# One list for all engines: the instructions of a decoder layer noted first, then put out in a searched sequence

## The chip, the cores and the metric

The kernel runs on one core of a Trainium2 chip. A core has five engines with an instruction stream each: TensorE (PE, matrix products, with its weight loads shown as PEld), VectorE (DVE), ScalarE (ACT), GpSimd (POOL) and SyncE (SP, which only issues transfers here). They meet through semaphores alone. The metric is the device time of one execution in microseconds (us); the profile shows one execution, instruction by instruction.

## The reference

One layer of a hybrid decoder: 512 tokens, width 1024, everything in float32. Three mixers run side by side (sliding-window attention, stick-breaking attention, attention to a memory of 256 rows), each through its own gate; then an output projection, a residual, and a gated feed-forward block of width 2816.

```
u = rms_norm(h, ln_mix_pre)
qa, ka, va, qb, kb, vb, qm, gl = split(u @ w_in)          # 1024 x 5888
y_swa = swa_sink_attention(qa, ka, va, sinks, rel_bias)   # 8 heads, window 128
y_sb  = stick_breaking_attention(qb, kb, vb)              # 8 heads
mk, mv = split(rms_norm(mem, ln_mem) @ w_mem_kv)
y_mem = memory_cross_attention(qm, mk, mv)                # 4 heads
g = sigmoid(gl)
merged = g0 * (y_swa @ w_branch_swa) + g1 * (y_sb @ w_branch_sb) + g2 * (y_mem @ w_branch_mem)
h = h + rms_norm(merged @ w_out, ln_mix_post)
u = rms_norm(h, ln_ffn_pre)
h = h + rms_norm((silu(u @ w_gate) * (u @ w_up)) @ w_down, ln_ffn_post)
```

## The kernel before

Every float32 factor is split into a high half (a cast, `hi`, on ACT) and the rest (a subtraction, `lo`, on DVE), and a product is three products of halves: hi by hi, hi by lo, lo by hi (`mm3`). The large products are done in seven partial products of 2 by 2 blocks; weight sums for these are made by accumulating transfers.

A `Stream` object carries a sequence of weight units. Each unit is loaded (512 KB to a `raw` tile, issued by SP or by POOL), split into `hi` and `lo`, and used by TensorE. Attention and the softmaxes are woven in between.

The function `tile_kernel` is run once to issue all instructions. The order in which it issues them is not the order in which the engines run them: the wrapper class `Noted` (through whose line 232 every instruction is issued, so that the profile gives one line for all of them) keeps each engine's instructions in a list `seen`, and at the end of `tile_kernel` a loop ties each engine's instructions into the sequence given by `ORDER`, a dictionary with one list for each engine, by dependencies that need no semaphore (`follow`). Numbers in `ORDER` count the instructions of that engine. `PLAN` says which buffer each tile takes: `raw`, `hi`, `lo`, `fraw`, `fhi`, `flo` for weights, `ck` and `ck2` for 512 and 1024 wide tiles, `p` and `p2` for the eight PSUM banks, `s` for small ones. Which instruction must wait for which is found in the order of issue, so a buffer's users follow one another in that order, whatever `ORDER` says.

The names that matter below, all at the start of the kernel unless said otherwise:

- `WARM` = 9 matrix products on constants open TensorE's stream.
- `first_load` and `first_split` load and split the first three weight units in four pieces (`PIECE`: 1, 2, 2 and 3 of the 8 columns of 128). ACT itself issues the first piece of units 0 and 2, then loads its function table (`preload_act_table_set`).
- `gain_split` makes the halves of one of the eight slices of the input, `u[k]`: times the gain, high half by ACT, low half by DVE. They are the tiles named pair; slice 0 comes with the gains in `xg` (the tile wide), the others in tiles named xT.
- `xacc` is the sum of squares; `rstd_of` splits it (`sh_x`, `sl_x`) and adds it up over partitions by two products with ones (`on_x`).
- Much later, in the memory branch, `mem_vals` multiplies halves of the memory (`mh`, `ml`) by weights `hi`, `lo`. `seven_raw` copies a head's output (`yq`), `parts` splits it (`y11h`, `y11l`).

Of the kernel before, what the change touches and what calls it, by code (L numbers as in the profile page):

```python
# [17 lines left out]
P = 128  # L18
# [19 lines left out]
ORDER = {  # L38
    "tensor": (
# [23 lines left out]
    ),  # L63
    "vector": (
# [81 lines left out]
    ),  # L146
}
PLAN = {
    "raw": (
# [2042 lines left out]
```

## Time and profile before

| | |
|---|---|
| median of 3 timed runs | 768.8 us (768.69 to 768.93) |
| profiled execution, first to last instruction (span) | 766.9 us |
| around the span: median less span | 1.9 us |
| mean granted TensorE clock | 0.997 |
| TensorE, weight loads | 99%, 84% of the span |
| DVE, ACT, POOL | 88%, 68%, 14% of the span |
| HBM read, written | 140.38 MB, 19.40 MB |

The page gives no time of its own for the profiled execution beside the span, so the timed runs stand for it. Of the 40 slices of the span only the last has TensorE below nine tenths. A TensorE instruction is listed from its start to the modelled end of its pipeline, so neighbours overlap; the distance of two starts is what one costs in the stream. "x8" in a row of the timeline means eight like instructions in a row.

### The profile page before, as it was taken

What the parts mean: (1) busy time and instruction counts of PE and PEld (TensorE: products, weight loads), DVE (VectorE), ACT (ScalarE), POOL (GpSimd) and SP (SyncE); (2) the same over time, 40 slices, a digit from 0 to 9 for tenths busy, and PEclk for the clock granted to TensorE, in tenths of its full rate; (3) what the DMA queues carried; (4) which work ended last, traced back from release to release, by engine and by line L of the source; (5) the groups of instructions that cost most, each with busy time, mean ns of one, the idle gap of its engine ahead of it and who ended that gap; (6) DMA issues with size and microseconds to landing.
All of it is one profiled execution on the core that took longest, in us unless ns stands there. A gap on an engine that the chain in (4) does not pass through costs nothing.

```text
span 766.9 us, 11497 instructions
## 1 busy us (share of the span) xinstructions
PE 759.1 (99%) x4073; PEld 647.3 (84%) x4073; DVE 675.2 (88%) x1100; ACT 520.3 (68%) x946; POOL 104.1 (14%) x140
## 2 busy tenths in 40 slices
PE   9999999999999999999999999999999999999996
PEld 6789888778888888888888899988888888888885
DVE  7994897799989756999897799899999999999966
ACT  7662677777997758677944596566666668957552
POOL 0303242000222110010001201100000000214000
PEclk9999999999999999999999999999999999999998
DMA  8548999734799895469949958876777746859922
GB/s 277 166 142 233 332 328 254 211 111 149 185 188 192 184 203 163 112 134 210 340 128 329 209 130 240 203 191 180 204 192 203 220 142 187 171 120 216 261 75 111
DMA packets 50170, 150.06 MB, mean 196 GB/s; under 512 B 5984, under 2 KB 7952, under 8 KB 50016
## 3 DMA queue, kind: packets, MB, share of 16 engines
q1 hardware_dynamic: 34224, 94.38, 36.8%
q0 software_dynamic: 15600, 54.80, 36.1%
q8 instruction: 32, 0.52, 0.3%
q14 instruction: 26, 0.21, 0.1%
q10 hardware_dynamic: 288, 0.13, 0.1%
HBM read 140.38 MB, written 19.40 MB: 208 GB/s over the span
## 4 chain that ended last, share of the span: by engine, by line
PE 96%; DMA 1%; DVE 1%; ACT 1%; issue 0%; SPq 0%; DVEq 0%
PE bank L232 96%; DMA xT<-in_xT 1%; DMA raw<-in_w_p 0%; DVE xacc L232 0%; SPq L232 0%; ACT pair L232 0%; DVE pair L232 0%; ACT hi L232 0%; ACT xT L232 0%; DVE lo L232 0%; DVE fg L232 0%; DVE sl_x L232 0%; DVEq L2180 0%; DVE s L232 0%; ACT sqr L232 0%
## 5 line engine op out<-in xcount | busy, mean ns | idle before, releaser
L232 PE MATMUL bank<-pair,hi 128*128 128x512 f32 (+1 forms) x1008 | 254.4, 368 | 0.0
L232 DVE TENSOR_TENSOR lo<-raw,hi 128x1024 fp32r<-128x1024 f32 (+4 forms) x149 | 170.7, 1149 | 36.8 <-ACT hi L232 36.2
L232 PEld LDWEIGHTS bank<-pair,hi 128*128 128x128 f32 x1008 | 177.5, 189 | 27.0 <-ACT hi L232 0.9
L232 ACT CAST hi<-raw 128x1024 fp32r<-128x1024 f32 (+4 forms) x149 | 147.7, 998 | 73.7 <-PE bank L232 54.5
L232 PE MATMUL bank<-hi,pair 128*128 128x512 f32 (+1 forms) x628 | 196.3, 374 | 0.0
L232 PE MATMUL bank<-pair,lo 128*128 128x256 f32 (+1 forms) x752 | 154.7, 302 | 0.0
L232 PEld LDWEIGHTS bank<-hi,pair 128*128 128x128 f32 x628 | 115.3, 188 | 19.5 <-issue 0.2
L232 PEld LDWEIGHTS bank<-pair,lo 128*128 128x128 f32 x752 | 115.6, 190 | 10.9 <-DVE lo L232 0.7
L232 PE MATMUL bank<-lo,pair 128*128 128x512 f32 (+1 forms) x330 | 123.6, 375 | 0.0
L232 ACT CAST hi<-wide 128x1024 fp32r<-128x1024 f32 (+1 forms) x61 | 62.2, 1024 | 27.0 <-PE bank L232 11.3
L232 DVE TENSOR_TENSOR lo<-wide,hi 128x1024 fp32r<-128x1024 f32 (+1 forms) x61 | 71.9, 1185 | 4.6 <-ACT hi L232 4.3
L232 PEld LDWEIGHTS bank<-lo,pair 128*128 128x128 f32 x330 | 62.0, 188 | 10.1
L232 POOL DMA_DIRECT2D raw<-in_w_g x24 | 21.1, 878 | 124.4 <-DVE lo L232 106.2
L232 DVE TENSOR_TENSOR gp<-gp,bank 128x512 f32<-128x512 f32 x49 | 33.6, 687 | 4.6 <-PE bank L232 3.7
L232 ACT ACTIVATE sg<-gp 128x256 f32<-128x256 f32 x42 | 17.7, 421 | 23.0 <-DVE gp L232 22.9
L232 POOL DMA_DIRECT2D raw<-in_w_gu x15 | 13.2, 924 | 147.6 <-DMA raw<-in_w_gu 138.5
L232 ACT COPY gp<-bank 128x512 f32<-128x512 f32 x42 | 24.7, 588 | 2.1 <-DVE aq L232 1.4
L232 DVE TENSOR_TENSOR_SCAN bw<-br,bw 128x512 f32<-128x512 f32 (+3 forms) x32 | 24.6, 809 | 0.2
L232 DVE TENSOR_TENSOR gp<-gp,hp 128x512 f32<-128x512 f32 x36 | 24.7, 685 | 0.0
L232 POOL DMA_DIRECT2D wide<-in_w_gu x12 | 11.2, 934 | 84.6 <-DMA wide<-in_w_gu 76.3
L232 ACT COPY hp<-bank 128x512 f32<-128x512 f32 x36 | 21.5, 598 | 0.0
L232 PE MATMUL bank<-hi,ll 128*128 128x512 f32 x50 | 19.4, 389 | 0.0
(624 smaller groups left out, 1371.8 us busy)
## 6 DMA issues: line engine op xcount, KB each, us to landing
wide<-in_w_gu SPq DMA_DIRECT2D x31, 512.0 KB, 5.1
raw<-in_w_gu SPq DMA_DIRECT2D x26, 512.0 KB, 5.4
raw<-in_w_g POOLq DMA_DIRECT2D x24, 512.0 KB, 6.0
raw<-in_w_g SPq DMA_DIRECT2D x18, 512.0 KB, 4.2
raw<-in_w_gu POOLq DMA_DIRECT2D x15, 512.0 KB, 7.2
raw<-in_w_p SPq DMA_DIRECT2D x14, 512.0 KB, 6.3
wide<-in_w_gu POOLq DMA_DIRECT2D x12, 512.0 KB, 5.8
raw<-in_w_brt SPq DMA_DIRECT2D x9, 512.0 KB, 4.8
```

The costliest lines, as they stand in the source:

```text
L232: ins = f(*args, **kw)
```

## The change

The operations, 6328 of them (4009 on TensorE, 1068 on DVE, 876 on ACT, 136 on POOL, 239 on SP), are the same. `Noted` goes. `Notes` only notes each call (`Op`) in one `Program`, tiles that don't exist yet are noted as `View`s, and at the end `put_out` issues all of them along one list, `ORDER`, whose numbers count the operations of all engines in the order of noting. Each engine is tied to that sequence as before, and waits are now found in the order of that list. A `ck` tile is made when its first user is put out. `ORDER` and all of `PLAN` are new; the `after`, `behind` and `high_priority` hints are taken out.

```
-ORDER = {
-    "tensor": (
-        "0-18 21 19-20 22-24 27 25-26 28-529 538-561 572-575 580-588 642 562-564 566-567 576-579 530-537 613-620 569 "
...
+ORDER = (
+    "15-16 12 18 17 19 13 1 3 33 35 37 40 263 2 4 20 639 36 39 24 0 21 5 34 339 303 335 25 196 371 267 22 631 299 "
+    "41 38 6-10 640 716 11 720 375 94 97 100 95 98 101 42-43 93 96 14 48-49 44-45 99 23 26 29 102 28 27 30 103 "
+    "192 105-107 104 31-32 90 193-194 74 46-47 108-110 50-51 111 114 117 112 115 118 113 116 119 75-76 56-59 "
...
+class Program:
+    def put_out(self, nc, order, follow):
+        real = lambda x: x.real() if isinstance(x, View) else x
+        last, out = {}, set()
+        for n in order or range(len(self.ops)):
+            op = self.ops[n]
+            assert all(b.at in out for b in op.behind)
+            out.add(n)
+            args = [real(x) for x in op.args]
+            ins = getattr(getattr(nc, op.engine), op.name)(*args, **{k: real(x) for k, x in op.kw.items()})
+            if op.engine in last:
+                follow(ins, last[op.engine])
+            last[op.engine] = ins
...
+class Notes:
...
         def call(*args, **kw):
-            ins = f(*args, **kw)
-            self.seen.append(ins)
-            return ins
+            op = Op(len(self.program.ops), self.engine, name, args, kw)
+            self.program.ops.append(op)
+            return op
...
         if kind == "ck" and n < SINGLES:
-            return pool.tile(shape, dt, tag=f"ck{n}", name=name, bufs=1)
+            return View(once(lambda: pool.tile(shape, dt, tag=f"ck{n}", name=name, bufs=1)))
...
-    for e, text in ORDER.items():
-        seen, last = getattr(nc, e).seen, None
-        for part in text.split():
-            a, _, b = part.partition("-")
-            for k in range(int(a), int(b or a) + 1):
-                if last is not None:
-                    follow(seen[k], seen[last])
-                last = k
+    order = []
+    for part in ORDER.split():
+        a, _, b = part.partition("-")
+        order += range(int(a), int(b or a) + 1)
+    program.put_out(tc.nc, order, follow)
```

The numbers of the list that are spoken of below, counted in the order of noting:

| numbers | operations |
|---|---|
| 3 to 11 | the nine warming products |
| 12, 13; 15, 16 | ACT's loads of piece 1 of units 0 and 2; SP's of `xg` and of piece 1 of unit 1 |
| 14 | ACT's function table |
| 33, 35, 37; 34, 36, 38 | casts of piece 1 of units 0, 1, 2; their low halves (128 wide) |
| 39 and 40; 41 | high half of `u[0]`, by DVE and by ACT; low half |
| 42, 44, 46; 43, 45, 47 | casts of piece 2 of units 0, 1, 2; their low halves (256 wide) |
| 48, 49; 50, 51 | `u[1]`, high and low; `u[2]`, high and low |
| 74 | the first square, to `xacc` |
| 93 to 101; 102 to 110 | products with `u[0]`; with `u[1]`, nine each |
| 165, 166; 167, 168 | `sh_x`, `sl_x`; the two products with ones |
| 1003, 1004; 1069, 1070 | cast and low half of one weight unit of `mem_vals`, and of the next |
| 1090, 1091; 1092, 1093 | `y11h`, `y11l`; the two copies `yq` of the same bank |
| 1154 | the first product that reads what 1004 wrote |

Set side by side, engine by engine, the two sequences differ little. Of TensorE's operations 1253 of 4009 keep their place and the mean distance is 3.8 places; on DVE 286 of 1068 and 1.9 places; on ACT 274 of 876 and 1.7. The products with ones go from places 81 and 82 of TensorE's stream to 95 and 96 (from 0). Runs of transposes among TensorE's products go from 42 to 83, for the same number of transposes; the places where a 256-wide product follows a 512-wide one go from 81 to 127. TensorE's last 25 products keep their sequence.

More of the change, by code (lines that the diff above doesn't have):

```diff
@@ L1 @@
 import math
-from contextlib import ExitStack, nullcontext
+from contextlib import ExitStack
 import numpy as np
@@ L220 @@
-class Noted:
-    def __init__(self, engine):
-        self.engine, self.seen = engine, []
+ORDER = (
[207 rows of a table added]
+)
+PLAN = {
+    "raw": (
+        "1 0 2 0 3 2 1 3 3 0 2 3 1 1 0 2 3 1 3 2 0 3 1 3 1 0 2 1 3 0 2 1 0 3 2 1 0 3 2 0 1 3 1 3 1 3 2 0 2 0 2 0 1 3 "
+        "2 0 1 3 2 0 1 0 1 0 1 3 2 0 1 3"
+    ),
+    "hi": (
+        "0 1 2 0 3 2 1 2 0 1 2 0 3 1 2 0 3 1 2 0 3 1 2 3 1 0 2 3 0 1 2 3 0 1 2 3 0 1 2 3 0 1 2 3 0 1 2 3 0 1 2 3 0 1 "
+        "2 3 0 1 2 3 0 1 2 3 0 1 2 3 0 1 2 0 3 1 2 0 3 0 1 2 3 0 1 2 3 0 1 2 3 0 1 2 3 0"
+    ),
+    "lo": (
+        "1 0 2 1 3 2 0 3 1 0 3 1 2 0 3 1 2 0 3 1 2 0 3 0 2 1 3 0 1 2 3 0 1 2 3 0 1 2 3 0 1 2 3 0 1 2 3 0 1 2 3 0 1 2 "
+        "3 0 1 2 3 0 1 2 3 0 1 2 3 0 1 2 3 1 0 2 3 1 0 1 2 3 0 1 2 3 0 1 2 3 0 1 2 3 0 1"
+    ),
[22 rows of a table added]
+    ),
[5 rows of a table added]
+    ),
+    "s": (
+        "0 1 4 2 5 3 6 8 10 7 9 11 12 13 15 14 4 3 0 2 5 1 6 10 11 7 8 9 14 13 12 15 3 2 4 5 0 10 6 7 11 8 1 13 9 15 "
+        "12 14 5 3 0 4 10 8 2 7 6 11 1 15 9 12 3 4 0 13 5 14 2 10 7 6 9 15 0 8 11 4 2 10 1 13 5 14 3 13 7 6 12 5 1 15"
+    ),
+    "spare": (
+        "7 6 5 4 0 1 2 3 2 3 7 6"
+    ),
+    "fraw": (
+        "3 2 1 4 8 7 5 6 0 2 3 8 4 1 7 4 2 0 6 8 5 7 3 0 4 1 8 4 3 2 6 1 5 7 4 2 0 3 8 6 7 1 6 5 8 2 0 4 1 3 7 6 5 4 "
+        "3 1 8 2 0 4 1 8 6 5 7 3"
+    ),
+    "fhi": (
[3 rows of a table added]
+    ),
+    "flo": (
[3 rows of a table added]
+    ),
+    "ck2": (
+        "1 12 13 9 5 4 6 2 11 8 0 7 10 3"
+    ),
+    "p2": (
+        "1 3 2 0 3 1 2 3 1 0 3 1 2 3 1 0 3 1 2 3 1 0 3 1 2 3 1"
+    ),
+}
@@ new lines, with __init__, then, __getitem__ @@
+class View:
+    def __init__(self, make, path=(), shape=None):
+        self.make, self.path, self.shape = make, path, shape
+    def then(self, f):
+        return View(self.make, self.path + (f,))
+    def __getitem__(self, k):
+        return self.then(lambda ap: ap[k])
+    def bitcast(self, dt):
+        return self.then(lambda ap: ap.bitcast(dt))
+    def rearrange(self, *args, **kw):
+        return self.then(lambda ap: ap.rearrange(*args, **kw))
+    def unsqueeze(self, axis):
+        return self.then(lambda ap: ap.unsqueeze(axis))
+    def to_broadcast(self, shape):
+        return self.then(lambda ap: ap.to_broadcast(shape))
+    def real(self):
+        ap = self.make()
+        for f in self.path:
+            ap = f(ap)
+        return ap
@@ new lines, with __init__ @@
+class Op:
+    def __init__(self, at, engine, name, args, kw):
+        self.at, self.engine, self.name, self.args, self.kw = at, engine, name, args, kw
+        self.behind = ()
+class Program:
+    def __init__(self):
+        self.ops = []
+    def put_out(self, nc, order, follow):
[10 more added lines that the diff above has]
+            last[op.engine] = ins
+        assert len(out) == len(self.ops)
@@ L256, in __getitem__, with once, f @@
         return self.held[c]
+def once(make):
+    got = []
+    def f():
+        if not got:
+            got.append(make())
+        return got[0]
+    return f
 class Places:
@@ L412, in dps @@
     def dps(name):
-        return places.take(psd, "p" if PLAN else "d", [P, 512], F32, name)
+        return places.take(psa, "p", [P, 512], F32, name)
     def aps(name):
-        return places.take(psa, "p" if PLAN else "a", [P, 512], F32, name)
+        return places.take(psa, "p", [P, 512], F32, name)
     def banks(name):
@@ L425, in split @@
         ins = nc.scalar.copy(hi, raw)
-        lows = nc.vector.tensor_tensor(lo, raw, hi.bitcast(F32), op=ALU.subtract)
-        if "behind" in st:
-            after(ins, st["behind"][0])
-            after(lows, st["behind"][1])
+        nc.vector.tensor_tensor(lo, raw, hi.bitcast(F32), op=ALU.subtract)
         return ins
@@ L441, in w_split @@
         uid[0] += 1
-        hi = places.take(wp, "hi", [P, 1024], F32R, f"hi{uid[0]}", bufs=4)
-        lo = places.take(wp, "lo", [P, 1024], F32R, f"lo{uid[0]}", bufs=4)
+        hi = places.take(wp, "hi", [P, 1024], F32R, f"hi{uid[0]}")
+        lo = places.take(wp, "lo", [P, 1024], F32R, f"lo{uid[0]}")
         if isinstance(raw, list):
             for i, x in enumerate(raw):
-                ins = split(x[:, :], hi[:, i * 512 : (i + 1) * 512], lo[:, i * 512 : (i + 1) * 512])
+                split(x[:, :], hi[:, i * 512 : (i + 1) * 512], lo[:, i * 512 : (i + 1) * 512])
         else:
-            ins = split(raw[:, :n], hi[:, :n], lo[:, :n])
-        if "chain" in st:
-            after(ins, st["chain"])
+            split(raw[:, :n], hi[:, :n], lo[:, :n])
         return hi, lo
@@ L456, in mm3 @@
         (lh, ll), (rh, rl) = l, r
-        one = nc.tensor.matmul(out, lh, rh, start=start, stop=False, skip_group_check=True)
+        nc.tensor.matmul(out, lh, rh, start=start, stop=False, skip_group_check=True)
         nc.tensor.matmul(out, lh, rl, start=False, stop=False, skip_group_check=True)
-        return one, nc.tensor.matmul(out, ll, rh, start=False, stop=stop, skip_group_check=True)
-    def mm3_behind(*args):
-        one, last = mm3(*args)
-        if "products" in st:
-            after(one, st["products"])
-        st["products"] = last
+        nc.tensor.matmul(out, ll, rh, start=False, stop=stop, skip_group_check=True)
     def mm(out, l, r, start, stop):
@@ L474, in tile_kernel @@
     pin, since = [], []
-    def after(ins, first):
-        if not ORDER:
-            follow(ins, first)
     def follow(ins, first):
@@ L486, in fn @@
         ins = nc.scalar.activation(*args, **kw)
-        for p in pin:
-            after(ins, p)
+        ins.behind = tuple(pin)
         since.append(ins)
@@ L494, in table, with const @@
         ins = nc.scalar.preload_act_table_set(name)
-        for x in since:
-            after(ins, x)
+        ins.behind = tuple(since)
         since.clear()
         pin[:] = [ins]
-    def const(name, shape, pool=cst):
-        t = places.fixed(cst, shape, F32, f"c_{name}") if pool is cst else pool.tile(shape, F32, name=f"c_{name}")
+    def const(name, shape, pool=None):
+        t = pool.tile(shape, F32, name=f"c_{name}") if pool else places.fixed(shape, f"c_{name}")
         nc.sync.dma_start(t[:, :], a[name])
@@ L796, in q_parts @@
                 h, l = cols(u[2 * c + k], 256, 256)
-                after(split(t[:, k * 256 : (k + 1) * 256], h, l), st["chain"])
+                split(t[:, k * 256 : (k + 1) * 256], h, l)
         else:
             h, l = qsum[(p, c)] = ck(f"xs{p}{c}h", F32R), ck(f"xs{p}{c}l", F32R)
-            ins = split(t[:, :], h[:, :], l[:, :])
-            if "chain" in st:
-                after(ins, st["chain"])
+            split(t[:, :], h[:, :], l[:, :])
     def q_left(p, c, k, i):
@@ L831, in q_end @@
             t = qkeep[(p, i)] = (spare if b == SWA and p in ("p1", "p6") else ck)(f"gq{b}{p}{i}")
-            st["chain"] = nc.scalar.copy(t[:, :], ps[:, :])
+            nc.scalar.copy(t[:, :], ps[:, :])
         if p == "p2":
@@ L862, in gen @@
                 for k in range(2):
-                    mm3_behind(qbank[key][:, :], q_left(p, c, k, i), cols((hi, lo), k * 512, 512), first and k == 0, c == 1 and k == 1)
+                    mm3(qbank[key][:, :], q_left(p, c, k, i), cols((hi, lo), k * 512, 512), first and k == 0, c == 1 and k == 1)
                 yield 1.36
@@ L937, in seven_end @@
             t = (ck if b == SB else spare)(f"s{p}{b}{i}")
-            with tc.high_priority():
-                nc.scalar.copy(t[:, :], ps[:, :])
+            nc.scalar.copy(t[:, :], ps[:, :])
             skeep[(p, i)] = t
@@ L971, in gen @@
                 for k in range(2):
-                    mm3_behind(sbank[i][:, :], seven_left(b, p, k, i), cols((hi, lo), k * 512, 512), first and k == 0, last and k == 1)
+                    mm3(sbank[i][:, :], seven_left(b, p, k, i), cols((hi, lo), k * 512, 512), first and k == 0, last and k == 1)
                 yield 1.36
@@ L1143, in tile_kernel @@
     raws = [places.take(wp, "raw", [P, 1024], F32, f"raw_first{i}") for i in range(FIRST)]
-    his = [places.take(wp, "hi", [P, 1024], F32R, f"hi_first{i}", bufs=4) for i in range(FIRST)]
-    los = [places.take(wp, "lo", [P, 1024], F32R, f"lo_first{i}", bufs=4) for i in range(FIRST)]
+    his = [places.take(wp, "hi", [P, 1024], F32R, f"hi_first{i}") for i in range(FIRST)]
+    los = [places.take(wp, "lo", [P, 1024], F32R, f"lo_first{i}") for i in range(FIRST)]
     def first_load(eng, p, units=range(FIRST)):
@@ L1210, in tile_kernel @@
-    pin[:] = [first_table]
+    idle = tc.nc.const_aps.tensor(1.0, [P, 512], BF16)
+    one_t = {}
+    for name in ("x", "m"):
+        one_t[name] = ck(f"on_{name}", F32R)[:, :P]
+        nc.vector.tensor_copy(one_t[name], idle[:, :P])
+    pw = dps("warm")
+    for i in range(WARM):
+        mm(pw[:, :], idle[:, :P], idle[:, :], True, True)
+    first_load(nc.scalar, 0, (0, 2))
+    first_table = nc.scalar.preload_act_table_set("natural_log_exp_and_others")
+    pin[:] = [first_table]
+    load_x(0, 1)
@@ new lines, in tile_kernel @@
+    first_load(nc.sync, 0, (1,))
+    load_x(1, 2)
+    first_load(nc.sync, 1, (0, 1))
+    load_x(2, 3)
+    first_load(nc.sync, 1, (2,))
+    first_load(nc.sync, 2, (0,))
+    load_x(3, 4)
+    first_load(nc.sync, 2, (1, 2))
+    load_x(4, 5)
+    first_load(nc.sync, 3)
+    load_x(5, 8)
+    dn.loaded = dn.have = FIRST
+    for p in range(len(PIECE)):
+        for i in range(FIRST):
+            first_split(i, p)
+        for k in range(*PIECE[p]):
+            gain_split(k)
+    xacc = ck("xacc")
@@ new lines, in tile_kernel @@
+    nc.scalar.activation(xacc[:, :], xraw[0][:, :], AF.Square)
+    for k in range(1, KC):
+        nc.scalar.activation(xraw[k][:, :], xraw[k][:, :], AF.Square)
+        nc.vector.tensor_tensor(xacc[:, :], xacc[:, :], xraw[k][:, :], op=ALU.add)
+    dn.ahead(4, 3)
+    for i in range(FIRST):
+        first_ps[("kb", i)] = aps(f"kb{i}")
+    order = [(i, 0, x) for x in ("hh", "lh", "hl") for i in range(FIRST)]
+    order += [(i, 1, x) for i in range(FIRST) for x in ("hh", "lh", "hl")]
+    for i, k, x in order:
+        w = (his if x[0] == "h" else los)[i]
+        mm(first_ps[("kb", i)][:, :], w[:, k * P : (k + 1) * P], u[k][x[1] == "l"], k == 0 and x == "hh", False)
@@ L1212, in tile_kernel @@
+    gens = [dn.units[i]["mm"](his[i], los[i]) for i in range(FIRST)]
+    for k in range(2, KC + 1):
+        for g in gens:
+            next(g, None)
+    dn.at = FIRST
+    st["rs"], st["rb"] = rstd_of("x", xacc, S, aps)
+    for f in st.pop("waiting"):
+        f()
     ident = const("ident", [P, P], base)
-    sinks = places.fixed(cst, [P, 8], F32, "sinks")
+    sinks = places.fixed([P, 8], "sinks")
     nc.sync.dma_start(sinks[:, :], a["sinks"].to_broadcast([P, 8]))
@@ L1401, in swa_pair @@
             pts[h] = [ck(f"pts{h}{i}") for i in range(2)]
-            with tc.high_priority():
-                nc.vector.tensor_copy(pts[h][0][:, P:], pt[h][0][:, P:])
-                nc.scalar.copy(pts[h][1][:, :], pt[h][1][:, :])
+            nc.vector.tensor_copy(pts[h][0][:, P:], pt[h][0][:, P:])
+            nc.scalar.copy(pts[h][1][:, :], pt[h][1][:, :])
         yield 2.0
@@ L1468, in tile_kernel @@
     sb_out(3)
-    st.pop("chain")
     table("natural_log_exp_and_others")
@@ L1580, in tile_kernel @@
     turned = {}
-    def behind(act, dve):
-        st["behind"] = (act, dve)
-    def ordered(act, dve):
-        if "behind" in st:
-            after(act, st["behind"][0])
-            after(dve, st["behind"][1])
-        return act, dve
     def place(name, t, src, sign=1.0):
@@ L1723, in seen @@
             return t[:, :].rearrange("p (j n) -> p j n", j=2)
-        def ordered_dve(ins):
-            if "behind" in st:
-                after(ins, st["behind"][1])
         def snap():
             t = ck(f"g{p}{n}")
-            ins = nc.scalar.copy(seen(t), main)
-            if "behind" in st:
-                after(ins, st["behind"][0])
+            nc.scalar.copy(seen(t), main)
             if wide:
@@ L1985, in tile_kernel @@
     dn.until(f"branch{MEM}")
-    if PLAN:
-        fp = None
-    else:
-        first.close()
-        fp = ctx.enter_context(tc.tile_pool(name="fp", bufs=9, reuse_waits="tile"))
+    fp = wp
     def f_split(raw, n):
         uid[0] += 1
-        hi = places.take(fp, "fhi", [P, 1024], F32R, f"hi{uid[0]}", bufs=4)
-        lo = places.take(fp, "flo", [P, 1024], F32R, f"lo{uid[0]}", bufs=4)
+        hi = places.take(fp, "fhi", [P, 1024], F32R, f"hi{uid[0]}")
+        lo = places.take(fp, "flo", [P, 1024], F32R, f"lo{uid[0]}")
         if isinstance(raw, list):
@@ L2065, in tile_kernel @@
     kept(1)
-    behind(since[-1], st["mixed"])
     table("silu_and_others")
@@ L2071, in tile_kernel @@
     go(3)
-    behind(*turn(3, tmp[3]))
+    turn(3, tmp[3])
     fs.hold = 5
@@ L2075, in tile_kernel @@
     turn_n2(2)
-    behind(*turn_n2(3))
+    turn_n2(3)
     fs.hold = 6
@@ L2079, in tile_kernel @@
     turn_n22(2)
-    behind(*turn_n22(3))
+    turn_n22(3)
     fs.hold = 8
@@ L2083, in tile_kernel @@
     for t in (2, 3):
-        late = turn_late(t, 0)
-    behind(*late)
+        turn_late(t, 0)
     fs.hold = 10
@@ L2089, in tile_kernel @@
         turn_late(t, 1)
-    st.pop("behind")
     fs.hold = 10**6
```

212 lines of the change are left out of this document (52 added, 160 removed), and 367 rows, old and new, of tables (ORDER, PLAN).

## Prediction

> **What bounds the kernel now.** First the page, for the shares of the engines, and the chain of the work that ended last:
>
> ```profile
> span 766.9 us, 11497 instructions
> PE 759.1 (99%) x4073; PEld 647.3 (84%) x4073; DVE 675.2 (88%) x1100; ACT 520.3 (68%) x946; POOL 104.1 (14%) x140
> ...
> 22.29 737.97 PE bank L232 x3990
> ```
>
> From 22.29 us on, for 737.97 us, to 760.26, the chain is TensorE alone, out of a span of 766.9 (the page counts TensorE before 22.29 as busy too). What is left is 22.3 us of head, which has products in it as well, and 6.7 us of tail. A busy TensorE need not be a TensorE that never waits, so next come TensorE's waits, and stretches in which its neighbours are differently loaded:
>
> ```profile
> PE bank L232 <- PEq L2174: 0.8, 1, 0.8
> PE bank L232 <- DVE sl_x L232: 0.4, 1, 0.4
> ...
> 700.00:725.00 25.00, 25.00 (x112) 20.69 (x111) 24.88 (x43) 15.79 (x28) 5.42 (x7) 1.00 1.00 248
> 725.00:750.00 25.00, 25.00 (x112) 20.71 (x111) 18.14 (x35) 14.62 (x29) 0.00 (x0) 1.00 0.26 85
> ```
>
> TensorE itself has two waits in the whole run, 0.8 us before its first instruction and 0.4 us for `sl_x`. And it takes 112 products in 25 us with DVE busy for 24.88 us and the transfer engines full (share 1.00), and 112 again with DVE at 18.14 and a share of 0.26. The pace is its own. A new sequence of the same products can't shorten that; it can only change what happens at the joints: the head, the changes between kinds of product, and waits that appear or go.
>
> **The change part by part.** Nothing is added and nothing removed: the table of the change has the same 6328 operations. So each part is a move, and the sum goes by TensorE's stream.
>
> *The head.* TensorE's start, then what feeds it:
>
> ```profile
> 0.78 4.00 PE L232 MATMUL bank<-const-bfloat16-1.0 128*128 128x512 bf16 x9 [0.78 <-PEq L2174]
> 4.75 1.02 PE L232 MATMUL bank<-pair,hi 128*128 128x512 f32 x3
> ...
> 7.87 0.39 PE L232 MATMUL bank<-pair,hi 128*128 128x512 f32 x1
> ...
> 21.54 0.39 PE L232 MATMUL bank<-sh_x,on_x 128*128 128x512 f32 x1
> 22.29 0.50 PE L232 MATMUL bank<-sl_x,on_x 128*128 128x512 f32 x1 [0.37 <-DVE sl_x L232]
> ```
>
> ```profile
> 1.66 1.28 ACT L232 ACT_TABLE_LOAD   x1 [1.66 <-PEq L2174]
> 4.00 0.51 ACT L232 ACTIVATE pair<-wide 128x256 fp32r<-128x256 f32 x1 [1.05 <-DMA wide<-in_xg]
> 4.41 0.68 ACT L232 CAST hi<-raw 128x128 fp32r<-128x128 f32 x3
> ...
> 5.63 0.73 ACT L232 ACTIVATE pair<-xT,wide 128x512 fp32r<-128x512 f32 x1
> 6.26 0.69 ACT L232 CAST hi<-raw 128x256 fp32r<-128x256 f32 x2
> ```
>
> ```profile
> 4.54 0.75 DVE L232 SCALAR_TENSOR_TENSOR pair<-wide,pair 128x512 fp32r<-128x512 f32 x1 [0.19 <-ACT pair L232]
> ...
> 8.44 0.42 DVE L232 TENSOR_TENSOR lo<-raw,hi 128x256 fp32r<-128x256 f32 x1
> ```
>
> ```profile
> 0.74 3.44 DMA raw<-in_w_p
> ...
> raw<-in_w_p ACTq DMA_DIRECT2D x2, 64.0 KB, 3.4
> ...
> raw<-in_w_p SPq DMA_DIRECT2D x1, 64.0 KB, 3.2
> ```
>
> Before, ACT loads its table in the dead time at 1.66, and makes its part of `u[0]` (40) as soon as `xg` is there, at 4.00, then the three casts; the first product starts at 4.75. The list has ACT do 33, 35, 37, then 40, 42, 14, 48. The first weights land at 0.74 + 3.44 = 4.18; the other two, issued some 0.45 us later, at about 4.4 and 4.6. The casts (three in 0.68) so end at about 4.85, 40 (0.51, started 0.1 before that) at 5.3, and the first product starts 0.1 later, at 5.4: **0.65 late**. Then the table: 42 ends at about 5.6 (a cast of 256 is half of 0.69 and a little), the load takes 1.28, to 6.9, and only then comes the high half of `u[1]` (48, 0.73), to 7.6. Its low half on DVE (49, 0.75) ends at 8.4, and behind it in DVE's sequence stands 45, the low half of unit 1's piece (0.42), at 8.8. Product 106, the 13th, needs that: it starts at about 8.85, where the 13th started at 7.87. So the head is **1.0 late** by then. From there the producers get ahead again (the last pieces are needed at 18 to 20 us and made by 17), and nothing is won back, since TensorE is never idle afterwards. What hid the table load was the wait for the first transfer; that cover is gone.
>
> On the other side, `sh_x` takes 0.75 us before where a product takes 0.23: the wait for `sl_x`. The list puts this pair 14 products (3.2 us) later. The wait goes, **-0.5**; if the sum of squares, late by the same table load, is also 3 us late, it stays, 0. I take -0.5.
>
> The Trainium skill, "ScalarE: Activation LUTs", section "What ACT_TABLE_LOAD costs", adds a drain of about 1380 ns to the 1283 ns of a load for a switch to another set. By it the head would lose an estimated 1.4 more and the sum below would be 771.0. The rows of a later switch decide, and there the next cast starts as the load ends:
>
> ```profile
> 152.06 1.28 ACT L232 ACT_TABLE_LOAD   x1
> 153.35 1.26 ACT L232 CAST qas<-qa 64x512 fp32r<-64x512 f32 x2
> ```
>
> *Transposes in more, shorter runs* (42 before, 83 in the list). Rows with a run of one and a run of six:
>
> ```profile
> 377.04 0.39 PE L232 MATMUL bank<-lo,pair 128*128 128x512 f32 x1
> ...
> 377.49 0.39 PE L232 MATMUL bank<-hi,pair 128*128 128x512 f32 x1
> 377.72 0.27 PE L232 MATMUL bank<-c_ident,gq2p 128*128 128x128 f32 x1
> 377.75 0.47 PE L232 MATMUL bank<-hi,pair 128*128 128x512 f32 x1
> 378.06 0.39 PE L232 MATMUL bank<-lo,pair 128*128 128x512 f32 x1
> 378.29 0.82 PE L232 MATMUL bank<-c_ident,gq2p 128*128 128x128 f32 x6
> 378.87 0.47 PE L232 MATMUL bank<-hi,ys2p3h 128*128 128x512 f32 x1
> 379.18 0.40 PE L232 MATMUL bank<-lo,ys2p3h 128*128 128x512 f32 x1
> ```
>
> From 377.04 to 377.72 three products take 0.68, 0.227 each. From 377.49 to 378.06 stand two products and one transpose: 0.57, less 0.454, is 0.116. From 378.06 to 379.18 two products and six transposes: 1.12 less 0.454 is 0.666, 0.111 each. So a run costs about 0.005 beside its transposes, and 41 more of them **0.2**; the rows are rounded to 0.01, so 0 to 0.8.
>
> *256-wide products* follow 512-wide ones at 127 places where there were 81:
>
> ```profile
> 562.21 1.11 PE L232 MATMUL bank<-pair,lo 128*128 128x256 f32 x8
> 563.16 2.00 PE L232 MATMUL bank<-pair,hi 128*128 128x512 f32 x8
> 565.00 1.11 PE L232 MATMUL bank<-pair,lo 128*128 128x256 f32 x8
> ```
>
> Eight narrow ones take 0.95, 0.04 over half of the wide pace (8 x 0.114), and the eight wide ones behind them 1.84, 0.02 over 8 x 0.227. A run cut in two may save half of its 0.04 or pay the 0.02 twice: 46 cuts, -0.9 to +0.9. Nothing says which; I take **0**.
>
> *The middle otherwise.* Operations move by 2 places on ACT and DVE and by 4 on TensorE, less than 1 us of stream, and the loads behind them by a few. Before, TensorE waited for none of them. I put **0.2** on new short waits; below, their bounds are 0 and 2.
>
> *The tail.* TensorE's last 25 products keep their sequence, and what follows them swaps two equal halves: 0.
>
> Sum: 1.0 - 0.5 + 0.2 + 0 + 0.2 = +0.9 on the profiled execution, 766.9 + 0.9 = 767.8 of span; the 1.9 us around it stay, so 768.8 + 0.9, about **769.6**, which a measurement of this kernel can't tell from no change (0.2% is 1.5 us: 767.3 to 770.3).
>
> **The rivals.**
>
> *The head costs nothing.* If the weights of the first pieces land as early as `xg`, ACT is not held up and the table load fits before the transfer of `u[1]`: then only the -0.5 and the small terms stay, 768.4. Against it: ACT's row at 4.00 and the landing at 4.18; before, ACT was busy without a gap from 4.00 on.
>
> *Slower: a split put just in time.* In the memory branch the list puts 1004, the low half of a weight, behind two others on DVE. The rows around it:
>
> ```profile
> 125.77 0.69 DVE L232 TENSOR_TENSOR y11l<-bank,y11h 128x512 fp32r<-128x512 f32 x1
> ...
> 126.50 0.65 ACT L232 COPY yq<-bank 128x256 f32<-128x256 f32 x2 [1.33 <-DVE y11l L232]
> 127.03 1.06 ACT L232 CAST hi<-raw 128x1024 fp32r<-128x1024 f32 x1
> ...
> 128.12 1.23 DVE L232 TENSOR_TENSOR lo<-raw,hi 128x1024 fp32r<-128x1024 f32 x1 [1.66 <-ACT hi L232]
> ...
> 130.63 0.39 PE L232 MATMUL bank<-lo,mh 128*128 128x512 f32 x1
> ```
>
> ACT's sequence there becomes `y11h` (to 125.1, as before), one copy `yq`, cast 1003, cast 1069, the other copy; DVE's is 1070, 1091, 1004. If the first copy no longer waits behind `y11l`, which now comes after it, it ends at 125.5, the casts at 126.5 and 127.5, the splits at 128.7, 129.4 (`y11l`) and 130.6, and product 1154 wants it at 130.63: no slack, no wait. If that copy still starts at 126.5, everything is 1.3 later and TensorE waits 1.3. The sum is then 769.6 + 1.3 = 770.9. It decides from 0.7 us on, which brings 770.3. For it: what slack 1004 had by standing ahead of the other two is spent. Against it: the same rows, with the copy first, just fit.
>
> *The change does nothing but re-sort* (head and runs as before, because the sequences stay near the old ones): 768.8. Against it are the moves in the head, which can be read off the list.
>
> *Much faster.* The Trainium skill, "TensorE: Matmul & The Clock Gate", section "Back-to-back issue gap", gives about 131 ns for each 512-wide product in a long stream of loads and products; this kernel's 227 ns would then leave room. As a mechanism here: if a pair's weight load hid better in another sequence, 1% of 738 us would be 7.4 us, 761.4 or so. The rows speak against it: 0.227 in every mix of neighbours above, whatever the loads.
>
> **How the numbers follow.** Forecast, 769.6, with its own range of 768.9 to 770.3: 0.47. Head free (768.4) or nothing but re-sorted (768.8): 0.20. Slower by a just-in-time wait (770.9, up to 772.5 if two such places meet): 0.29. Much faster: 0.04. Same sign: within 0.2% are the first two, less an edge, 0.66; slower 0.30; faster 0.04, since without a new pace only the 0.5 us of `sl_x` can be won. The range runs from 768.0, the free head with its small terms at their low side, to 772.5.
>
> **What would show it.** After: the first real product near 5.4 and the 13th near 8.85; ACT's table load at about 5.6; no wait for `sl_x`, and the pair at about 25.5; 112 products in 25 us as before; TensorE's waits few, the first of them for `lo` in the memory branch near 131. I am wrong if the first product starts by 4.8, if TensorE shows several waits over 0.5 us between 30 and 760 us, or if 25 us hold more than 112 wide products.

## The result, and the profile after

The change makes the kernel slower by 10.3 us: 779.1 us (median, 777.92 to 779.48) against 768.8 (768.69 to 768.93), a ratio of 1.0131 with a 95% interval of 1.0117 to 1.0146. The forecast was 769.6, its range ended at 772.5. One later execution, the first of experiment e11, was disturbed (2048 us) and is left out.

The page of after, span and engines:

```profile
span 777.3 us, 11469 instructions
...
PE 764.7 (98%) x4073; PEld 645.7 (83%) x4073; DVE 680.6 (88%) x1100; ACT 518.5 (67%) x947; POOL 105.5 (14%) x140
```

The span grew by 10.4. The products are the same 4073; ACT has one instruction more, a function table load that is not in the list (below). Two windows of 25 us late in the run, to set beside those of before (length; busy time of PE, PEld, DVE, ACT and POOL with the number of instructions; clock, share of the transfer engines, GB/s):

```profile
700.00:725.00 25.00, 25.00 (x112) 20.68 (x111) 22.41 (x34) 17.28 (x28) 9.63 (x11) 1.00 1.04 217
725.00:750.00 25.00, 25.00 (x111) 20.57 (x111) 24.47 (x43) 15.10 (x28) 0.00 (x0) 1.00 0.58 162
```

112 and 111 products, as before: the pace is untouched, and the 10 us are at the joints. TensorE's waits say at which (what was waited for; us in total, times, longest):

```profile
PE bank L370 <- ACT pair L370: 1.5, 1, 1.5
PE bank L370 <- DVE w L370: 1.1, 1, 1.1
PE bank L370 <- DVE bw L370: 1.0, 2, 0.9
PE bank L370 <- DVE eps_t L370: 0.8, 1, 0.8
PE bank L370 <- PEq L2257: 0.8, 1, 0.8
```

The wait for `sl_x` is gone; four of 0.8 to 1.5 us have come. The one for `eps_t` is the head (a small DVE operation that happened to end last ahead of the first product); the others are in the middle. First the head, on TensorE and then on ACT:

```profile
0.78 4.00 PE L370 MATMUL bank<-const-bfloat16-1.0 128*128 128x512 bf16 x9 [0.78 <-PEq L2257]
5.61 0.76 PE L370 MATMUL bank<-pair,hi 128*128 128x512 f32 x1 [0.83 <-DVE eps_t L370]
6.17 0.63 PE L370 MATMUL bank<-pair,lo 128*128 128x512 f32 x1
6.59 1.05 PE L370 MATMUL bank<-pair,hi 128*128 128x512 f32 x2
...
8.73 0.59 PE L370 MATMUL bank<-pair,lo 128*128 128x512 f32 x1
9.15 0.63 PE L370 MATMUL bank<-pair,hi 128*128 128x512 f32 x2
9.62 0.40 PE L370 MATMUL bank<-pair,lo 128*128 128x512 f32 x1
```

```profile
1.66 1.28 ACT L370 ACT_TABLE_LOAD   x1 [1.66 <-PEq L2257]
3.94 0.72 ACT L370 CAST hi<-raw 128x128 fp32r<-128x128 f32 x3 [1.00 <-DMA raw<-in_w_p]
...
5.39 1.28 ACT L370 ACT_TABLE_LOAD   x1
```

The first real product starts at 5.61, and from there to 9.15 products start 0.427 apart, the pace of the warm-up products, where before they had about 0.23 from the second on. The table load of the list stands at 5.39; the one at 1.66 was put in by the compiler, since a cast now comes ahead of the list's (with before's head, in e3 and e5 below, there are nine loads again and not ten). By its 41st product, warm-up included, TensorE is 2.17 late (14.41 against 12.24).

Then the middle. The largest waits, as the time from one product's start to the next over what the same neighbours usually take in both traces: 1.04 at 91.9 and 0.34 at 101.4 (`bw`), 1.27 at 203.2 and 0.28 at 222.2 (`w`), 2.4 between 443.9 and 447.8 (`pair`), 0.24 at 190.7, 0.49 at 611.7. What is behind the first, in before:

```profile
81.09 0.48 ACT L232 ACTIVATE t_m<-bank,eps_t 128x256 f32<-128x256 f32 x1 [1.37 <-PE bank L232]
```

```profile
81.69 0.42 DVE L232 TENSOR_SCALAR v_m<-bank 128x256 f32<-128x256 f32 x1
```

and in after, ACT, DVE and TensorE:

```profile
84.28 0.47 ACT L370 ACTIVATE t_m<-bank,eps_t 128x256 f32<-128x256 f32 x1 [2.55 <-DVE v_m L370]
...
85.23 1.28 ACT L370 ACT_TABLE_LOAD   x1
```

```profile
81.11 2.35 DVE L370 TENSOR_TENSOR lo<-raw,hi 128x1024 fp32r<-128x1024 f32 x2
83.37 0.55 DVE L370 TENSOR_SCALAR wide<-bank,wide 128x320 f32<-128x320 f32 x1
83.83 0.41 DVE L370 TENSOR_SCALAR v_m<-bank 128x256 f32<-128x256 f32 x1
```

```profile
91.79 0.38 PE L370 MATMUL bank<-c_ident,bw 128*128 128x128 f32 x2
93.05 0.66 PE L370 MATMUL bank<-c_ident,bw 128*128 128x128 f32 x3 [0.87 <-DVE bw L370]
```

`t_m` (ACT) and `v_m` (DVE) read the same PSUM bank, and neither needs the other. In before `t_m` goes first. In after ACT sits idle for 2.55 us, the last 1.5 of them with the sum in the bank, until `v_m` has been, and `v_m` stands on DVE behind two splits of 1.2. The table load, the exponentials and `bw` behind it come late. The sequences of ACT and DVE alone don't show this: it is the list that has 671 (`v_m`) ahead of 670 (`t_m`), far ahead in time of the place where DVE gets to it.

This is a rule throughout. In after, 97 reads by ACT or DVE come in the list behind a read of the other engine of the same bank, with no new product in the bank in between. None of them started before that other read had ended. Taken in the order of noting, 14 of 106 did. In before, by the order of noting, none of 106 did. The Trainium skill, "PSUM — Partial Sum Buffer", section "PSUM bank collisions raise a hardware error", says that the compiler's scheduler ties any two instructions of different engines on the same 32 partitions of one bank to each other, reads with reads too; the traces agree. So who reads first is part of the sequence, and over the whole run such reads stood held for 12.6 us in after and for 2.4 in before (only those held longer than 0.15, beyond what their own operands and engine asked).

A read can also be held without a turned pair. Fifteen pairs stand in the list against the order of noting, but only four of them are among the eleven reads that were held longer than 0.15. The longest wait, at 443.9, has ACT's copies 3512 and 3516 behind DVE's reads 3511 and 3515 of the same banks, in both lists in that order. The change puts 3511 four and 3515 ten places later on DVE, among splits of 1.2. On ACT, DVE (3515) and TensorE in after:

```profile
440.41 0.65 ACT L370 CAST pair<-bank 128x256 fp32r<-128x256 f32 x2 [2.06 <-DVE pair L370]
443.34 0.37 ACT L370 CAST pair<-bank 128x256 fp32r<-128x256 f32 x1 [2.29 <-PE bank L370]
```

```profile
442.83 0.42 DVE L370 TENSOR_TENSOR pair<-bank,pair 128x256 fp32r<-128x256 f32 x1
```

```profile
445.68 0.39 PE L370 MATMUL bank<-pair,hi 128*128 128x256 f32 x1 [1.51 <-ACT pair L370]
```

The profile puts the second wait of ACT down to TensorE; it ends 0.09 after DVE's read, and with that read behind it (e2 below) it is gone.

### The profile page after: what moved, and what is told of

Same layout as the page of the kernel before. It is cut to its first block, busy times and chain, and to the rows that moved or that the text cites. A ratio compares the mean times of both kernels' runs of the same rounds, so it can differ in the third digit from the quotient of the medians.

```text
span 777.3 us, 11469 instructions
## 1 busy us (share of the span) xinstructions
PE 764.7 (98%) x4073; PEld 645.7 (83%) x4073; DVE 680.6 (88%) x1100; ACT 518.5 (67%) x947; POOL 105.5 (14%) x140
## 4 chain that ended last, share of the span: by engine, by line
PE 88%; DVE 5%; ACT 4%; issue 1%; DMA 0%; DVEq 0%; ACTq 0%
PE bank L370 88%; DVE lo L370 1%; DVE w L370 1%; ACT w L370 1%; ACT hi L370 1%; DVE bw L370 1%; DVE pair L370 1%; ACT xq L370 1%; ACT pair L370 0%; DMA raw<-in_w_p 0%; DVE s L370 0%; ACT sp L370 0%; ACT mt L370 0%; ACT L370 0%; DVE yq L370 0%
## 5 line engine op out<-in xcount | busy, mean ns | idle before, releaser
L370 PE MATMUL bank<-hi,pair 128*128 128x512 f32 (+1 forms) x702 | 211.9, 378 | 0.0
L370 DVE TENSOR_TENSOR lo<-raw,hi 128x1024 fp32r<-128x1024 f32 (+4 forms) x154 | 175.9, 1150 | 29.9 <-ACT hi L370 26.3
L370 PEld LDWEIGHTS bank<-pair,hi 128*128 128x128 f32 x983 | 172.3, 190 | 29.4 <-ACT pair L370 1.9
L370 PEld LDWEIGHTS bank<-hi,pair 128*128 128x128 f32 x702 | 129.0, 188 | 23.9 <-ACT wide L370 0.5
L370 PE MATMUL bank<-lo,pair 128*128 128x512 f32 (+1 forms) x366 | 133.4, 377 | 0.0
L370 PEld LDWEIGHTS bank<-lo,pair 128*128 128x128 f32 x366 | 68.3, 188 | 11.6 <-DVE lo L370 0.2
L370 ACT CAST hi<-wide 128x1024 fp32r<-128x1024 f32 (+1 forms) x56 | 56.9, 1020 | 21.2 <-PE bank L370 9.0
L370 DVE TENSOR_TENSOR lo<-wide,hi 128x1024 fp32r<-128x1024 f32 (+1 forms) x56 | 65.9, 1180 | 4.4 <-ACT hi L370 4.4
L370 PE MATMUL bank<-pair,pair 128*128 128x512 f32 (+1 forms) x180 | 47.5, 368 | 0.0
L370 PEld LDWEIGHTS bank<-pair,pair 128*128 128x128 f32 x180 | 31.5, 188 | 6.0 <-issue 0.3
```

The costliest lines, as they stand in the source:

```text
L370: ins = getattr(getattr(nc, op.engine), op.name)(*args, **{k: real(x) for k, x in op.kw.items()})
```

## The experiments

Theory: the head (late start, then half pace) costs 2.2 us, and reads of one bank that go in the list's order cost some 5 of the 8 in the middle. Rivals: the way of putting out from one list costs it; the new sequences of ACT and DVE as such cost it; TensorE's new sequence does. All kernels were timed in five rounds beside before, except e14, which ran once for its profile.

**e1, before's sequences through the new way.**

```diff
-ORDER = ( the searched list )
-PLAN = the new buffers
+ORDER = ( before's five sequences, merged by the start times of before's trace )
+PLAN = before's buffers
```

> The sequences and the buffer plan of before, each engine's as it was, written as one list and put out by the changed kernel's way, its waits found in the order of the list (which is that of before's own trace). Theory (the sequence costs it: head and held reads): nothing of the 10.3 us comes back, 768.8, within 0.5. Rival (the way of putting out costs it, by other waits, by the table load that the compiler may add, or by tiles that are released in another order): most of the 10.3 us is here too, 774 to 779.

Measured: 768.5 (768.23 to 768.83), ratio to before 0.9997 (0.9988 to 1.0006). Noting, one list and waits in its order cost nothing; what costs is the list.

**e2, only whose read comes first.** Each engine's sequence and all buffers stay. For eleven held reads the other engine's read is moved behind them in the list. Four of these pairs so come back to the order of noting; the other seven, those of 443.9 among them, now go against it. The second of them is `t_m`:

```diff
- ... 669 671 654 682 686 638 646 687-689 679-680 724 684-685 651 670 683 ...
+ ... 669 654 682 686-689 679-680 724 684-685 651 670-671 638 646 683 ...
```

> The changed kernel with each engine's sequence and every buffer as they are; only in the list, between the engines, the ten-odd reads that stood held behind another engine's read of the same PSUM bank (t_x, t_m, y01l, the copies of pair, five more) are put ahead of that other read. Theory (two engines' reads of one bank go in the order of the list, and where the list puts first the read whose engine comes late, the other waits and TensorE behind it): the waits at 91.9, 101.4, 203.2 and 443.9 to 447.8 go, 1.04 + 0.12 + 0.34 + 1.27 + 1.76 + 0.67, in all 5.2 of the 779.1: 773.9, from 773 to 775.5. Rival (the new sequences of ACT and DVE use up the slack, whatever the reads' order): 779.1, within 0.7.

Measured: 774.6 (774.35 to 775.66). No instruction has changed its place on any engine, and 4.5 of the 10.3 us are gone. On ACT and DVE:

```profile
83.09 0.47 ACT L362 ACTIVATE t_m<-bank,eps_t 128x256 f32<-128x256 f32 x1 [1.09 <-PE bank L362]
```

```profile
84.11 0.41 DVE L362 TENSOR_SCALAR v_m<-bank 128x256 f32<-128x256 f32 x1
...
198.53 0.69 DVE L362 TENSOR_TENSOR pair<-bank,y01h 128x512 fp32r<-128x512 f32 x1
```

`t_m` now starts as soon as its product is there, and `y01`'s low half follows its engine at once, where after had it behind a copy on ACT:

```profile
200.62 0.69 DVE L370 TENSOR_TENSOR pair<-bank,y01h 128x512 fp32r<-128x512 f32 x1 [1.51 <-ACT yq L370]
```

The waits of the expectation are gone, but two new ones stand at 175.5 (0.56) and 443.5 (0.90). In both a read that goes first makes the other engine late: at 175.5 the copy 1371, which e2 put first; at 443.5 the copy 3616, which the change had put first and e2 left there.

**e3, the head of before; e4, both.** e3 has before's first 36 operations on TensorE, 19 on ACT, 20 on DVE and 16 on SyncE, for instance on ACT:

```diff
-ACT: 12 13 33 35 37 40 42 14 48 44 74 46 50 ...
+ACT: 12 13 14 40 33 35 37 74 48 42 44 50 46 ...
```

> The changed kernel with the head in before's sequence: TensorE's first 36, ACT's first 19, DVE's first 20 and SyncE's first 16 operations; all else as changed. Theory (the late start also brings TensorE back to half pace for eight products, so that the head costs 2.2 by its 40th product): first real product at 4.75 with no slow products behind it, 776.9. Rival (only the late start counts, my forecast's 1.0): 778.1. Rival (the head is regained at the first later wait, 91.9, where TensorE waits for DVE anyway): 779.1.

> Both of the edits before in one kernel. Theory (both costs stand by themselves, one behind the other in TensorE's stream): 779.1 - 2.2 - 5.2 = 771.7, from 770.9 to 773; 1 to 3 us then are still over before, from the places 190.7, 222.2 and 611.7 and small waits. Rival (the sequences cost it): 776.9, the head alone. Rival (the gains don't add, one wait takes the place of the other): 773.5 or more.

Measured: e3 776.8 (776.72 to 777.04), 2.3 gained, the theory's 2.2 and not the forecast's 1.0; the waits of the middle come 2.1 sooner and are as long as in after. e4 773.3 (772.89 to 773.49), over the 771.7 expected and its range: the two new waits of e2, 1.5 in all, are in it too. In the traces the gains add: from the 40th to the last product e2 and e4 take the same 751.99. The median of e2 lies 1.0 lower than that would have it, since its executions fall apart, three at 774.4 to 774.6 and two, the traced one among them, at 775.5 to 775.7.

**e5, two of the reads chosen again.**

```diff
- ... 3660-3662 3616 3611 ...      (the copy ur10 ahead of pair7's low half)
+ ... 3660-3662 3611 3616 ...
```

and the copy of `yq111` (1371) again behind `y13`'s low half (1369), as in the changed kernel.

> The kernel with before's head and the reads put back, with two of the reads set otherwise: the copy of yq111 again goes behind y13's low half as in the changed kernel, and the low half of pair7 now goes ahead of the copy ur10, as in before. Theory (a read put first is paid by the other engine: these two choices made the new waits of 0.56 + 0.10 at 173.5 and of 0.90 at 441.6): both waits go, 773.3 - 1.5 = 771.8, from 771.2 to 772.6. Rival (the waits there come from the sequences, the reads' order only moves them): 773.3, within 0.6.

Measured: 771.8 (771.64 to 772.04), as expected. So 2.3 us are the head and 5.0 the order of reads, and 3.1 are left. TensorE's waits:

```profile
PE bank L361 <- PEq L2248: 0.8, 1, 0.8
PE bank L361 <- ACT gp L361: 0.3, 1, 0.3
```

**e12, the other way round:** before's sequences and buffers, with three of the changed kernel's reads.

```diff
-670 ahead of 671, 1663 ahead of 1664, 3611 ahead of 3616
+671 ahead of 670, 1664 ahead of 1663, 3616 ahead of 3611
```

> The sequences and buffers of before as one list, with three reads set as the changed kernel has them: v_m ahead of t_m, the copy yq000 ahead of y01's low half, the copy ur10 ahead of pair7's low half. Theory (the order of the reads costs by itself): t_m 1.0 late, which its 1.5 us of slack takes; y01's low half 3.2 late, of which the softmax behind it on DVE has 0.65 of slack: 2.5; pair7's low half 1.0 late with no slack: 1.0. So 768.6 + 3.5 = 772.1, from 770.5 to 773. Rival (it costs only together with the new sequences): 768.6, within 0.5.

Measured: 773.7 (773.18 to 774.19), 5.0 slower than before, a little over the range. The order of reads costs by itself. The waits came as worked out (2.37 at the softmax, 1.01 at `pair7`, and 0.39 where nothing was expected), and something more came behind the first of them:

```profile
199.44 0.39 PE L402 MATMUL bank<-hi,ys1p3l 128*128 128x512 f32 x1
202.04 0.70 PE L402 MATMUL bank<-c_ident,w 128*128 128x128 f32 x4 [2.21 <-DVE w L402]
202.50 0.64 PE L402 MATMUL bank<-lo,ys1p6h 128*128 128x512 f32 x1
202.94 1.05 PE L402 MATMUL bank<-hi,ys1p6l 128*128 128x512 f32 x2
...
205.50 0.77 PE L402 MATMUL bank<-c_ident,w 128*128 128x128 f32 x3
205.99 0.51 PE L402 MATMUL bank<-pair,hi 128*128 128x512 f32 x1
```

From 202.5 to 205.9 products of 512 start 0.427 apart: half pace, after a wait of 2.2 us, for 3.4 us. Eight such products at 0.2 more than usual are about 1.5 us, and with it the parts come to 5.3. The granted clock shows it too (windows; the number before the last two is the clock):

```profile
202.50:206.00 3.50, 3.50 (x13) 2.72 (x12) 3.39 (x8) 1.45 (x4) 0.00 (x0) 0.52 0.52 199
```

**e6, e7, e8, the half pace by itself.** More warm-up products in the changed kernel, fewer in before's sequences (the numbers in the list moved accordingly):

```diff
-WARM = 9
+WARM = 13      (e6, changed kernel);  7 (e7) and 8 (e8), before's sequences
```

> The changed kernel with 13 warm-up products in place of 9, so that TensorE is not idle ahead of the first real one. Theory (after some 4 us of work TensorE goes to full pace, and about 1 us of idleness sends it back for 3.5 us): the warm-up products from about the tenth on take 0.22 and the first real ones, near 5.6, 0.227; 779.1 - 8 x 0.2 = 777.4, from 777.0 to 778.0. Rival (the eight products are slow for what goes on beside them, transfers, casts, weights): they keep 0.427, 779.1.

> The sequences of before as one list, with 7 warm-up products in place of 9: TensorE is idle from about 3.7 to 4.75, 1.0 us, as long as in the changed kernel. Theory (idleness sends it back to half pace): some eight real products of 0.427 from 4.75 on, 768.5 + 1.6 = 770.1, from 769.5 to 770.8. Rival (the half pace in the changed kernel has to do with what runs beside it): 768.5, within 0.5.

> The same with 8 warm-up products: idle from about 4.15 to 4.75, 0.6 us. Theory as stated says nothing of the length that it takes; if 0.6 is enough, 770.1 as with 7, if not, 768.5 with full pace from the first product or soon after. Rival (what runs beside it): 768.5.

Measured: e6 778.2 (777.84 to 778.36), e7 769.7 (768.95 to 770.17), e8 768.7 (768.36 to 768.94). The heads of e6 and e7:

```profile
0.78 5.70 PE L362 MATMUL bank<-const-bfloat16-1.0 128*128 128x512 bf16 x13 [0.78 <-PEq L2249]
5.92 0.89 PE L362 MATMUL bank<-pair,hi 128*128 128x512 f32 x1
6.65 0.39 PE L362 MATMUL bank<-pair,lo 128*128 128x512 f32 x1
```

```profile
0.78 3.15 PE L402 MATMUL bank<-const-bfloat16-1.0 128*128 128x512 bf16 x7 [0.78 <-PEq L2289]
4.63 1.65 PE L402 MATMUL bank<-pair,hi 128*128 128x512 f32 x3 [0.71 <-ACT hi L402]
...
10.47 0.85 PE L402 MATMUL bank<-pair,hi 128*128 128x512 f32 x3
```

With no pause ahead of them the real products of e6 have full pace from 6.65, in the same surroundings of casts and transfers in which after's went at half pace; with a pause of 0.9 us before's own go at half pace until 10.25. So the pause does it, not what runs beside it; 0.5 us (e8) does not. The sizes were off: full pace did not come after a set 4 us (e6's last four warm-up products still took 0.427 each), so e6 gained 0.9 in place of 1.7, and e7 lost 1.0 in its median where 1.6 were expected. Its profiled execution shows eleven slow products and not eight; it is the slowest of the eleven that were timed (768.95 to 770.17).

**e9, e10, TensorE's sequence of before** with the rest of the change (e9), and with head and reads of e5 (e10):

```diff
-TensorE: the list's 4009
+TensorE: before's 4009 (buffers, ACT, DVE, SyncE as in the list)
```

> The changed kernel (its buffers, its sequences on ACT, DVE and SyncE, its order of reads) with TensorE's whole sequence from before. Theory (the waits come from what ACT and DVE deliver late, and TensorE's own new sequence costs only its 0.3 us of shorter runs): 778.6, from 777.6 to 779.6. Rival (TensorE's new sequence asks for operands earlier than they can be there, and that is what made the waits): 774 or less.

> The kernel with before's head and the reads put back (771.8), with TensorE's whole sequence from before as well; what is left of the change are the sequences of ACT, DVE and SyncE behind the head and the buffers. Theory (the last 3 us are small waits for these engines): 771.4, from 770.8 to 772. Rival (the last 3 us belong to TensorE's sequence): 769.0 or less.

Measured: 793.1 (791.36 to 794.66) and 787.1 (786.93 to 787.29). Both theories missed by far. The longest of e9's new waits:

```profile
PE bank L340 <- ACT hi L340: 2.5, 2, 1.6
PE bank L340 <- ACT pair L340: 1.5, 1, 1.5
PE bank L340 <- ACT sh_x L340: 1.4, 1, 1.4
```

TensorE's new sequence doesn't make the waits: with the new ones on ACT and DVE it is 14.0 faster than before's (779.1 against 793.1). The sequences differ by a few places, but they are made for one another, and here half of a set is worse than either.

**e11, e14, one gain of the change by itself:** the pair of products with ones 14 products later, in before's sequences.

```diff
-TensorE: ... 164 167 168 206 207 ...
+TensorE: ... 164 206 207 ... (14 products) 167 168 ...
```

> The sequences of before as one list, with the pair of products for the sum of squares 14 products later, as the changed kernel has it. Theory (TensorE's 0.6 us wait for the low half of the sum goes and nothing else changes): 768.0, from 767.5 to 768.5. Rival (the sum is late whenever it is wanted, or what follows it is late in its place): 768.6 or more.

> The sequences of before with the pair of products for the sum of squares 14 products later, once more for its profile. Theory (the scales 1/rms come 3.2 us later, ACT and DVE can't empty the first banks until then, and TensorE waits for a bank): the wait for the sum's low half is gone and one or more waits of 1 to 3 us stand between 25 and 40 us. Rival (the later products come out with the half pace again): eight to sixteen products of 0.427 in the same stretch.

Measured: e11 771.0 (median of six, 770.08 to 772.21; interval of the ratio 1.0020 to 1.0042), e14 772.3. The 0.6 us of `sl_x` are saved and more is lost. In e14's timeline:

```profile
50.93 0.31 PE L402 MATMUL bank<-hi,pair 128*128 128x320 f32 x1
53.06 0.42 PE L402 MATMUL bank<-hi,pair 128*128 128x320 f32 x1 [1.82 <-DVE qb L402]
...
54.74 0.47 PE L402 MATMUL bank<-lo,pair 128*128 128x320 f32 x1
55.01 0.73 PE L402 MATMUL bank<-hi,pair 128*128 128x320 f32 x2
```

The scales come 3.0 later, DVE empties `qb`'s banks later, and TensorE waits 2.0 for one, at 51 and not between 25 and 40; and from 54.5 to 57.9 products of 320 start 0.267 apart, not 0.147. Both expectations had half of it. The six of e11 lie in two groups, three at 770.1 to 770.4 and three at 771.7 to 772.2. Their distance of about 1.7 is near what e14's slow stretch costs (3.4 us at 0.267 for 0.147: 1.5, an estimate), so it may be that only half of the executions have that stretch; those of e11 have no trace that shows it.

**e13, three copies one place sooner**, on the kernel of e5, on ACT:

```diff
-... 1625 1598 ...   ... 2501 2523 ...   ... 5563 5084 ...
+... 1598 1625 ...   ... 2523 2501 ...   ... 5084 5563 ...
```

> The kernel with before's head and the reads put back (771.8), with three of ACT's copies one place sooner: sp111 ahead of pts11, one of y's quarter banks ahead of the last softmax weight, gp18 ahead of the cast lh3. Theory (the last 3 us are waits of 0.1 to 0.6 us for a bank whose copy stands one place too late on ACT): 0.24 + 0.11, 0.12 + 0.1 and 0.49 + 0.10 go, 771.8 - 1.1 = 770.7, from 770.3 to 771.3. Rival (the operations that change places with them are wanted as soon, or the 3 us are not in such waits): 771.8, within 0.4.

Measured: 771.5 (771.19 to 771.63), 0.3 of the 1.1 expected. The waits at 605 and 188 are gone, but 0.27 for a softmax weight at 189.0 and 0.11 at 312 have come in their place. TensorE's list of waits now names only its start, and 2.8 us over before are left. In the trace 2.2 of them lie behind the 41st product. Set against what the same neighbours usually take (an estimate), they are 0.3 in the mix of neighbours, 0.6 more in starts that are over 0.1 us late (1.2 without before's `sl_x`), 0.8 in those of 0.03 to 0.1, 0.5 in smaller ones. Which single operations stand for these, and what part the new buffers have, stays open: no run has the old buffers with the new sequences.

## Why the prediction was wrong

| step | forecast | in the trace | by experiment |
|---|---|---|---|
| head | +1.0 | +2.17 | 2.3 (e3) |
| wait for `sl_x` | -0.5 | -0.65 | not to be had alone (e11) |
| transposes in more runs, 256-wide | +0.2 | +0.28 | |
| new short waits | +0.2 (0 to 2) | +8.55 | 5.0 the order of reads (e5), some 3.5 the rest |
| tail | 0 | 0 | |
| sum | +0.9 | +10.35 | 10.3 |

The trace's numbers are taken from the starts of products: up to the 41st, and behind it (755.81 against 747.62, 8.19 = 0.28 - 0.65 + 8.55, rounded). The 0.28 is an estimate from what the same neighbours usually take, and the 8.55 is what it leaves; 5.0 and 3.5 are differences of medians and of this row.

*What held.* The late first product (5.4 forecast, 5.61), the table load in the way (5.6, 5.39), the end of the `sl_x` wait, the price of shorter runs, the unchanged pace, the tail.

*Where it failed.* The step "the middle otherwise": operations move by 2 places on ACT and DVE, so less than 1 us, so 0.2. What came were 8.55 us. The step failed twice. It took the change for five sequences. A list over all engines also says in which order two engines touch the same bank, and this can't be seen in a place on one engine: 671 stands one place sooner on DVE and 670 in its old place on ACT, and 671 ahead of 670 in the list holds ACT for 1.5. The list stood in the change, with 15 pairs of such reads turned against the order of noting; they were not looked for beyond one place. And it took a mean for the largest: 23 operations of DVE and 7 of ACT move by ten places or more, and 3515 on DVE, one of them, holds ACT at the longest wait, 1.76 us of TensorE.

*The rival that was nearest* had the mechanism and the wrong place: the copy `yq` and `y11`'s low half on one bank, 1.3 at 131. There the reads were turned as well, and TensorE waited for nothing; it waited at other places, at 91.9, 101.4 and 203.2 behind turned reads and at 443.9 behind reads in their old order. Its chance (0.29) and its end (772.5, two such places) were too low for the same reason: one place was weighed, where all 15 pairs and the far moves could have been.

*The head*: the late start was right (0.65 forecast, 0.86 measured), the size of the whole was not. The term lacked the half pace, 8 products of 0.2 us. Its second part, the load that delays operation 45, cost nothing: 45 ends at 8.55, as forecast (8.8), but the 13th real product, which needs it, starts at 10.08 only. Before's trace has the cover in it: nine warm-up products that end 0.2 us ahead of the first real one. A first product that comes 0.9 later leaves them too short by 0.9, and that is a price of the pause itself, beside the delay.

Two small sums were off as well: 768.8 + 0.9 is 769.7, and a free head is 768.7 by its own terms (768.8 - 0.5 + 0.2 + 0.2), not 768.4. Beside 10.3 neither matters.

## What to carry to other kernels

When streams are written out over all engines, the order of two engines' reads of one PSUM bank is part of the schedule, and it can be changed without moving any instruction on its engine: look for reads that an engine idles on although their operand is there, and put first the one whose engine is there first. And look at the operations that move farthest, not at the mean. A sequence is a set: one engine's half of another schedule, or one move out of it, may cost more than either whole (e9, e11). Whatever searches such lists should know of all this and of TensorE's pace after a pause; how this list was found, and what that search knew, is not shown here.

## What the runs showed of the hardware that was not expected

TensorE's half pace comes back. The trace keeps records of the clock, from its first rise to full on. In the head that rise depends on the pause between the warm-up products and the first real one (from start to start, less the 0.427 of a warm-up product). In eleven profiled executions with a pause of about 0.5 us or less (before, e1, e3 to e6, e8, e10, e12, e13, e14) the first record begins at 4.0 to 6.7 us, at a different time in each. With 0.9 to 1.1 (after, e2, e7, e9) it begins at 9.1 to 10.1: 4.90 in before, 9.14 in after, where the starts pass from 0.427 to 0.227. The windows show no half clock there, since they count full clock ahead of the first record:

```profile
5.60:9.10 3.50, 3.49 (x8) 2.66 (x9) 2.48 (x7) 3.18 (x6) 2.71 (x5) 1.00 1.06 354
```

These are eight products in 3.5 us, at a clock that is given as 1.00; ahead of the first record only the distance of starts tells.

In the middle, half clock for 3.4 us followed waits of 2.0 us (e14) and 2.4 us (e12), 1.4 and 0.6 us after they ended, and in e9 and e10 two waits of 1.6 and 1.1 us close together. It didn't follow single waits of 0.9 to 1.8 us (after, at 91.9, 203.2 and 443.9; e9, ahead of 382.3 and 458.5). In all records, each stretch between two changes of the clock is a whole number of 3.413 us: 222 of them in before, 224 in after, one in each of the slow stretches. So the changes come in steps of that length, and where the steps fall differs from execution to execution. The Trainium skill, "TensorE: Matmul & The Clock Gate", section "Part 1: The HAM clock gate", describes a free-running window of activity of about 3.4 us, and that the number of slow products differs from run to run; the length of 3.4 us and the scatter agree with it, while waits of 2.0 us, shorter than that window, were enough here.

Neither engine is the one to read first as a rule: e2 turned the first read over to the other engine at eleven places, and at one of them (175.5) the engine that had been first then was the late one, for 0.56 us of TensorE.
